# Loading the old state of an mLSTM layer in whole-sequence pieces, one step ahead of its products

## The chip, the core and the metric

The kernel runs on one core of a Trainium2 chip. The metric is the device time of one execution in microseconds (us), the median of a few runs. The engines named below are TensorE (PE, with its weight loads PEld), VectorE (DVE), ScalarE (ACT), GpSimd (POOL) and SyncE (SP), whose queue issues most of the loads from memory.

## What is computed

The reference is one inference step of a two-layer trunk, for a prompt of 512 tokens and 8 sample sequences of 4 tokens (544 columns together): a half-step feed-forward block, a mixer, another half-step block, per layer. The mixer of the first layer is an mLSTM with 4 heads of width 512; that of the second is a chunked gating MLP. What the change touches is one term of the mLSTM, for the 8 sample sequences, which carry an old state C0 of 512x512 per sequence and head:

```python
def _mlstm_chunk(C0, n0, m0, q, k, v, ig, lf):
    ...
    num = (jnp.einsum('bhts,bshe->bthe', sc, v)
           + jnp.einsum('bthd,bhde->bthe', q, C0) * w_inter.transpose(0, 2, 1)[..., None])
    ...
    h = num / den
```

The einsum of q and C0 is what the text calls q C0. For each of 4 heads and 8 sequences it reads 1 MB of state, 32 MB in all.

## The kernel before

Each layer's activations lie as 8 tiles of 128 channels by 544 columns. A large product is made as three products of rounded parts: each weight tile of 128x1024 is loaded into a buffer `raw` (512 KB), split by ACT into a high part `whi` (L274) and by DVE into a low part `wlo` (L275), and then used by 48 products of `mm3` (L260). There are two buffers each of `whi` and `wlo`, and six of `raw` (`RAW = 6`). A `raw` buffer comes free when the split of its tile is done.

The mLSTM has a first phase (`phase_a`) and a second (`phase_b`). The first has 16 steps, one for each tile of the up-projection: step i loads and multiplies the i-th tile of `in_ml_up`, runs the convolution and the small projections of the tile before (`post`), and then pops two jobs from the list `self.units`. The sixteen gate tiles (`z_tile`, the second half of `in_ml_up`, here z0 to z15) follow: z0 at the end of the first phase, the rest as steps `z1` of the second, in an order that is written out by hand. Its beginning, for the first head, is

```python
B_FIRST = ("u2 z1 z1 z1 z1 g1 u1 u2 u1 u1 z1 z1 z1 s1 u2 u1 u1 z1 z1 u2 u2 z1 z1 z1 a3 u1 s1 u1 u2 q0 z1 s1 q1 "
```

where `u1` pops one job of `self.units`, `u2` two, `z1` makes a gate tile, `g1` turns the gate rows into columns (`columns`, L1051 to L1064), `s1` makes a step of the sample part and `q0` one of the prompt part.

`self.units` holds the q C0 work, 19 jobs for each head (`sample_units`, L1137): a `begin` that loads the head's q and lays it out in `qpad` as 4 x 8 tiles of 128x32 columns, two empty jobs, and 16 units. A unit takes one sequence b and half of the state's row tiles: it loads two row tiles of 128x512 (512 KB) into a buffer of the same six as the weights (`c0`, L1152; the trace calls it `c`) and makes two fp32 products (L1157), each with 32 columns of output on a column group of its own (`tile_position=(0, 32 * dt)`). They add up in one PSUM tile over the eight sequences. The last unit of a head also copies the PSUM tile out.

Outside the feed-forward blocks the order of instructions on an engine isn't the order of the program word for word: when the program is built, an instruction whose inputs would not be there yet lets ready ones of its engine go ahead, and a buffer is given to the first in the program that waits for it. Each product of L1157 shows as two records in the trace, since fp32 runs in two passes.

Of the kernel before, what the change touches and what calls it, by code (L numbers as in the profile page):

```python
# [10 lines left out]
F32 = mybir.dt.float32  # L11
# [7 lines left out]
P = 128  # L19
# [11 lines left out]
RAW = 6  # L31
# [148 lines left out]
class Trunk:  # L180
# [956 lines left out]
    def sample_units(self, h):  # L1137

        nc, a = self.nc, self.a
        s = {}  # L1140

        def begin():
            qk = self.mc.tile([P, 4, NS], F32, tag="qu", name="qu", bufs=1)
            nc.sync.dma_start(out=qk, in_=self.aux_d[h][:, :, :NS])
            for e in range(4):
                q = self.qpad[:, e].rearrange("p b t -> p (b t)")
                dg = bass.AP(q.tensor, q.offset, [list(q.ap[0]), [NS + 4, 8], [1, 4]])
                nc.gpsimd.tensor_copy(out=dg, in_=qk[:, e, :].rearrange("p (b t) -> p b t", t=4))
            s["qc"] = self.st()

        def unit(b, d2):
            c0 = self.wp.tile([P, 1024], F32, tag="raw", name="c0", bufs=RAW).rearrange("p (d e) -> p d e", d=2)  # L1152
            dsl = slice(2 * d2 * P, (2 * d2 + 2) * P)
            nc.sync.dma_start(out=c0, in_=a["sC"][b, h, dsl].rearrange("(d p) e -> p d e", p=P))
            for dd in range(2):
                dt = 2 * d2 + dd
                nc.tensor.matmul(out=s["qc"][32 * dt:32 * dt + 32, :], lhsT=self.qpad[:, dt, b, :], rhs=c0[:, dd, :],  # L1157
                                 start=b == 0, stop=b == 7, tile_position=(0, 32 * dt))

        def end():  # L1160
            t = self.com.tile([P, NT], F32, tag="sq", name="qct", bufs=2)[:, :512]
            nc.scalar.activation(out=t, in_=s["qc"], func=AF.Copy)
            nc.scalar.dma_start(out=self.qc_d[h], in_=t)

        jobs = [begin] + 2 * [lambda: None] + [lambda b=b, d2=d2: unit(b, d2) for b in range(8) for d2 in range(2)]

        def last(w=jobs[-1]):
            w()
            end()
        return jobs[:-1] + [last]  # L1170
# [458 lines left out]
```

## Time and profile before

| | us |
|---|---|
| median of 3 runs | 2242.74 |
| lowest run | 2239.98 |
| the profiled execution | 2241.03 |
| its span, first to last instruction | 2239.3 |
| PE busy in the span | 2196.3 |

What lies outside the span is 1.7 us. The highest of the three runs is 7586.79 us, an outlier. Busy times are unions over an engine's instructions; a matmul's end is modelled, so that neighbours overlap a little. In a timeline a row is a stretch of like instructions: start, length, engine, line, shape and how many of them.

### The profile page before, as it was taken

To read this page: it belongs to the slowest core of one execution; us is meant where nothing else is said; L and a number is where in the kernel's file an instruction comes from. 1 tells how busy PE (TensorE), PEld (TensorE's weight loads), DVE (VectorE), ACT (ScalarE), POOL (GpSimd) and SP (SyncE) were. 2 spreads that over 40 slices of the span, in tenths; PEclk is the share of its full clock that TensorE was granted. 3 is DMA by queue.
4 is the path that set the end of the run, shared out by engine and by line. 5 is a ranking of instruction groups with operands and counts; after the bars stand their busy time and mean duration, and the time that the engine had idled before them with its cause. 6 is when DMAs were issued, how large, how long until landed. Compare 5 with 4: busy or idle time off the path is not lost.

```text
span 2239.3 us, 42182 instructions
## 1 busy us (share of the span) xinstructions
PE 2196.3 (98%) x17056; PEld 2096.5 (94%) x17056; DVE 1601.2 (72%) x2271; ACT 1094.1 (49%) x1646; POOL 357.9 (16%) x499
## 2 busy tenths in 40 slices
PE   7999999999999999999999999999999999999997
PEld 7999999888987789899999999999999999999997
DVE  7989887544356676898998756555565567988885
ACT  6655655444455453665655542132224445665654
POOL 0111111332111100011111011121112100111110
PEclk9999999999999999999999999999999999999999
DMA  5677774576767653367777557876874224676772
GB/s 168 158 196 166 174 180 127 177 231 216 260 225 258 222 183 111 83 155 188 167 186 178 149 194 247 291 255 213 294 233 160 79 75 100 159 196 165 177 177 64
DMA packets 176603, 405.17 MB, mean 181 GB/s; under 512 B 18224, under 2 KB 47232, under 8 KB 176408
## 3 DMA queue, kind: packets, MB, share of 16 engines
q1 hardware_dynamic: 119296, 299.10, 41.6%
q0 software_dynamic: 36560, 79.12, 17.4%
q10 hardware_dynamic: 20552, 24.26, 3.0%
q8 instruction: 134, 2.20, 0.4%
q14 instruction: 61, 0.50, 0.1%
HBM read 342.60 MB, written 59.81 MB: 180 GB/s over the span
## 4 chain that ended last, share of the span: by engine, by line
PE 91%; DVE 4%; ACT 2%; DMA 2%; issue 1%; POOL 0%; SPq 0%; POOLq 0%; ACTq 0%; DVEq 0%
PE set L157 44%; PE mm L260 34%; PE mm L1364 2%; PE s L1157 2%; PE s L1327 1%; PE s L1291 1%; PE s L929 1%; PE mm L739 1%; PE s L260 1%; PE s L1550 1%; DMA xs<-xsd 1%; PE s L1478 0%; PE s L1274 0%; DMA vd<-vt 0%; DVE xt L157 0%
## 5 line engine op out<-in xcount | busy, mean ns | idle before, releaser
L274 ACT ACTIVATE whi<-raw 128x1024 fp32r<-128x1024 f32 (+2 forms) x148 | 151.5, 1024 | 468.0 <-PE mm L260 353.9
L260 PE MATMUL mm<-xgh,whi 128*128 128x272 f32 x1616 | 339.7, 291 | 1.0 <-DVE xm L249 1.0
L260 PE MATMUL mm<-xgl,whi 128*128 128x272 f32 x1616 | 335.8, 289 | 1.0 <-DVE xgl L157 0.9
L260 PE MATMUL mm<-xgh,wlo 128*128 128x272 f32 x1616 | 334.4, 288 | 1.3 <-DVE wlo L275 1.3
L157 PE MATMUL set<-xsh,whi 128*128 128x272 f32 x1056 | 305.4, 289 | 12.9 <-ACT whi L157 9.5
L157 PE MATMUL set<-xsl,whi 128*128 128x272 f32 x1056 | 304.4, 288 | 0.9 <-DVE xsl L157 0.9
L157 PE MATMUL set<-xsh,wlo 128*128 128x272 f32 x1056 | 304.2, 288 | 0.8 <-DVE wlo L157 0.8
L157 DVE TENSOR_TENSOR wlo<-raw,whi 128x1024 fp32r<-128x1024 f32 (+2 forms) x205 | 226.8, 1106 | 80.3 <-ACT whi L157 80.2
L260 PEld LDWEIGHTS mm<-xgh,whi 128*128 128x128 f32 x1616 | 254.0, 188 | 19.9 <-issue 15.5
L260 PEld LDWEIGHTS mm<-xgl,whi 128*128 128x128 f32 x1616 | 253.6, 188 | 1.9 <-DVE xgl L157 1.9
L260 PEld LDWEIGHTS mm<-xgh,wlo 128*128 128x128 f32 x1616 | 252.8, 188 | 2.1 <-DVE wlo L275 1.6
L157 ACT ACTIVATE whi<-raw 128x1024 fp32r<-128x1024 f32 (+2 forms) x205 | 197.9, 965 | 81.0 <-PE set L157 68.4
L157 ACT ACTIVATE set<-set 128x272 f32<-128x272 f32 x285 | 108.8, 382 | 239.6 <-PE set L157 235.5
L157 PEld LDWEIGHTS set<-xsh,whi 128*128 128x128 f32 x1056 | 199.0, 188 | 14.0 <-ACT whi L157 9.5
L275 DVE TENSOR_TENSOR wlo<-raw,whi 128x1024 fp32r<-128x1024 f32 (+2 forms) x148 | 176.4, 1192 | 42.5 <-ACT whi L274 39.1
L157 PEld LDWEIGHTS set<-xsh,wlo 128*128 128x128 f32 x1056 | 199.4, 189 | 1.4 <-DVE wlo L157 1.4
L157 PEld LDWEIGHTS set<-xsl,whi 128*128 128x128 f32 x1056 | 199.4, 189 | 1.1 <-DVE xsl L157 1.1
L157 PE MATMUL set<-xsh,whc 128*128 128x272 f32 x584 | 169.8, 291 | 1.6 <-ACT whc L157 1.6
L157 PE MATMUL set<-xsh,wlc 128*128 128x272 f32 x584 | 169.3, 290 | 0.7 <-DVE wlc L157 0.7
L157 PE MATMUL set<-xsl,whc 128*128 128x272 f32 x584 | 169.7, 291 | 0.0
L157 PE MATMUL set<-hl,whi 128*128 128x272 f32 x496 | 143.7, 290 | 0.0
L157 PE MATMUL set<-hh,wlo 128*128 128x272 f32 x496 | 142.9, 288 | 0.0
(387 smaller groups left out, 5363.9 us busy)
## 6 DMA issues: line engine op xcount, KB each, us to landing
raw<-in_ffn_gate SPq DMA_DIRECT2D x88, 512.0 KB
raw<-in_ffn_up SPq DMA_DIRECT2D x88, 512.0 KB
c<-in_sC SPq DMA_DIRECT2D x64, 512.0 KB
c<-in_sC SPq DMA_DIRECT2D x32, 1024.0 KB
out_Cs<-c POOLq DMA_DIRECT2D x32, 1024.0 KB, 6.8
raw<-in_ffn_down SPq DMA_DIRECT2D x80, 384.0 KB
raw<-in_ml_up SPq DMA_DIRECT2D x32, 512.0 KB
raw<-in_ffn_up POOLq DMA_DIRECT2D x60, 256.0 KB, 5.9
```

The costliest lines, as they stand in the source:

```text
L157: r = f(*args, **kw)
L260: nc.tensor.matmul(out=ps[h], lhsT=w[:, wsl], rhs=x[:, h * HN:(h + 1) * HN], start=k == 0 and q == 0, stop=k == n - 1 and q == 2)
L274: nc.scalar.activation(out=hi, in_=src, func=AF.Copy)
L275: nc.vector.tensor_tensor(out=lo, in0=src, in1=hi.bitcast(F32), op=ALU.subtract)
L739: nc.tensor.matmul(out=ps[:, pi, :HN], lhsT=w[:, w0:w0 + P], rhs=h[pi], start=z == 0, stop=z == 6 * nj - 1)
L929: nc.tensor.matmul(out=ps[:, tt * P:(tt + 1) * P], lhsT=t[:, tt * P:(tt + 1) * P], rhs=wd[w], start=True, stop=True)
L1157: nc.tensor.matmul(out=s["qc"][32 * dt:32 * dt + 32, :], lhsT=self.qpad[:, dt, b, :], rhs=c0[:, dd, :], start=b == 0, stop=b == 7, tile_po ...
L1291: nc.tensor.matmul(out=ps[:, :n], lhsT=kk[:, i * P:(i + 1) * P], rhs=qq[:, i * P:NP], start=z == 0, stop=z == 11)
L1327: nc.tensor.matmul(out=ps, lhsT=s_[:, c], rhs=v_[:, i], start=i == 0 and q == 0, stop=i == T and q == 2)
L1364: nc.tensor.matmul(out=ps, lhsT=kk[:, tt], rhs=vv[:, tt], start=tt == 0 and q == 0, stop=tt == 3 and q == 2)
L1550: nc.tensor.matmul(out=ps[r], lhsT=s["ks"][v][rows, dsl], rhs=s["vs"][rows], start=True, stop=True, tile_position=(32 * r, 0))
```

## The change

The 16 units of a head become 8 pairs of jobs, `load` and `unit`, one pair for each sequence. `load` takes two of the six buffers and loads all four row tiles into them; `unit`, the next job in the list, makes the four products, one after the other, on the four column groups. A head still has 19 jobs, so the places in the hand-written order stay; as two jobs are popped in each step of the first phase, a load there stands one step before its unit.

```diff
-        def unit(b, d2):
-            c0 = self.wp.tile([P, 1024], F32, tag="raw", name="c0", bufs=RAW).rearrange("p (d e) -> p d e", d=2)
-            dsl = slice(2 * d2 * P, (2 * d2 + 2) * P)
-            nc.sync.dma_start(out=c0, in_=a["sC"][b, h, dsl].rearrange("(d p) e -> p d e", p=P))
-            for dd in range(2):
-                dt = 2 * d2 + dd
-                nc.tensor.matmul(out=s["qc"][32 * dt:32 * dt + 32, :], lhsT=self.qpad[:, dt, b, :], rhs=c0[:, dd, :],
+        def load(b):
+            s["c0"] = []
+            for d2 in range(2):
+                c0 = self.wp.tile([P, 1024], F32, tag="raw", name="c0", bufs=RAW).rearrange("p (d e) -> p d e", d=2)
+                dsl = slice(2 * d2 * P, (2 * d2 + 2) * P)
+                nc.sync.dma_start(out=c0, in_=a["sC"][b, h, dsl].rearrange("(d p) e -> p d e", p=P))
+                s["c0"] += [c0[:, 0, :], c0[:, 1, :]]
+
+        def unit(b):
+
+            for dt, c0 in enumerate(s["c0"]):
+                nc.tensor.matmul(out=s["qc"][32 * dt:32 * dt + 32, :], lhsT=self.qpad[:, dt, b, :], rhs=c0,
                                  start=b == 0, stop=b == 7, tile_position=(0, 32 * dt))
...
-        jobs = [begin] + 2 * [lambda: None] + [lambda b=b, d2=d2: unit(b, d2) for b in range(8) for d2 in range(2)]
+        jobs = [begin] + 2 * [lambda: None] + [lambda f=f, b=b: f(b) for b in range(8) for f in (load, unit)]
```

## Rows read from the trace of the kernel before

**Rows 1.** The page's busy times of PE and PEld over the span, the slices of PE and of the granted clock, and the two heads of the chain that ended last, by engine and by line.

```profile
PE 2196.3 (98%) x17056; PEld 2096.5 (94%) x17056; DVE 1601.2 (72%) x2271; ACT 1094.1 (49%) x1646; POOL 357.9 (16%) x499
...
PEclk9999999999999999999999999999999999999999
...
PE 91%; DVE 4%; ACT 2%; DMA 2%; issue 1%; POOL 0%; SPq 0%; POOLq 0%; ACTq 0%; DVEq 0%
```

**Rows 2.** Busy time of each engine in two stretches that hold all of the q C0 products, first of all instructions, then of line 1157 alone. Columns: length, then busy us and instructions of each engine, granted clock, share of the DMA engines, GB/s.

```profile
425.00:560.00 135.00, 134.49 (x1119) 112.75 (x1119) 62.25 (x113) 58.81 (x82) 41.21 (x103) 1.00 0.69 221
560.00:800.00 240.00, 237.14 (x1653) 195.54 (x1653) 134.03 (x277) 115.05 (x198) 31.53 (x62) 0.99 0.70 235
...
425.00:560.00 135.00, 13.85 (x80) 2.36 (x80) 1.00 0.69 221
560.00:800.00 240.00, 27.88 (x176) 5.46 (x176) 0.99 0.70 235
sum 375.00, PE 41.73 PEld 7.82; mean PE 20.86 PEld 3.91
```

**Rows 3.** Whom PE waited for from 425 to 800 us: us in total, times, longest.

```profile
PE s L1327 <- ACT hn L1330: 2.1, 1, 2.1
PE mm L1364 <- ACT cst L1367: 0.7, 1, 0.7
PE s L1157 <- POOL qpad L1148: 0.5, 1, 0.5
```

**Rows 4.** PE's timeline at six places: stretches of q C0 records (line 1157) of different length, for three of them with what follows.

```profile
687.69 1.04 PE L1157 MATMUL s<-c,qpad 128*32 128x512 f32 x2
...
513.89 1.05 PE L1157 MATMUL s<-c,qpad 128*32 128x512 f32 x4
...
441.46 1.06 PE L1157 MATMUL s<-c,qpad 128*32 128x512 f32 x8
442.46 0.52 PE L260 MATMUL mm<-xgh,whi 128*128 128x272 f32 x2
...
451.24 1.06 PE L1157 MATMUL s<-c,qpad 128*32 128x512 f32 x8
452.23 0.52 PE L260 MATMUL mm<-xgh,whi 128*128 128x272 f32 x2
...
461.69 1.04 PE L1157 MATMUL s<-c,qpad 128*32 128x512 f32 x6
462.66 0.44 PE L949 MATMUL s<-con,qkvs 128*128 128x128 f32 x2
463.03 1.04 PE L1157 MATMUL s<-c,qpad 128*32 128x512 f32 x2
464.01 0.52 PE L260 MATMUL mm<-xgh,whi 128*128 128x272 f32 x2
...
741.42 1.92 PE L1157 MATMUL s<-c,qpad 128*32 128x512 f32 x16
```

**Rows 5.** One step of the first phase: SP's issues of weight tiles and state pieces, and the split of the weight tile that was issued at 442.58 us (ACT for the high part, DVE for the low one). What PE does at 452.23 and 464.01 stands in the group above.

```profile
441.12 0.37 SPq L1154 DMA_DIRECT2D c<-in_sC  x1
442.58 0.34 SPq L212 DMA_DIRECT2D raw<-in_ml_up  x1
443.01 8.24 SPq L1154 DMA_DIRECT2D c<-in_sC  x2
452.33 0.34 SPq L212 DMA_DIRECT2D raw<-in_ml_up  x1
...
448.54 1.06 ACT L274 ACTIVATE whi<-raw 128x1024 fp32r<-128x1024 f32 x1 [4.23 <-PE mm L260]
...
449.63 1.23 DVE L275 TENSOR_TENSOR wlo<-raw,whi 128x1024 fp32r<-128x1024 f32 x1
```

**Rows 6.** The place in the second phase around `g1`: SP's issues, the two splits by ACT and by DVE, and PE from the last gate-row transposes to the next gate tile.

```profile
543.26 14.00 SPq L1154 DMA_DIRECT2D c<-in_sC  x4
562.77 0.34 SPq L212 DMA_DIRECT2D raw<-in_ml_up  x1
...
569.83 0.33 SPq L212 DMA_DIRECT2D raw<-in_ml_up  x1
...
567.48 1.06 ACT L274 ACTIVATE whi<-raw 128x1024 fp32r<-128x1024 f32 x1 [0.46 <-ACT sz L1113]
...
561.54 1.20 DVE L275 TENSOR_TENSOR wlo<-raw,whi 128x1024 fp32r<-128x1024 f32 x1
...
568.58 1.23 DVE L275 TENSOR_TENSOR wlo<-raw,whi 128x1024 fp32r<-128x1024 f32 x1 [2.26 <-ACT whi L274]
...
571.36 0.38 PE L1059 MATMUL s<-con,r_rep 4*128 4x4 f32 x4
571.67 2.77 PE L1157 MATMUL s<-c,qpad 128*32 128x512 f32 x20
574.37 0.52 PE L260 MATMUL mm<-xgh,whi 128*128 128x272 f32 x2
```

**Rows 7.** Whom SP's queue waited for, in the whole span: its state pieces (L1154) and its weight tiles (L212), us in total, times, longest.

```profile
SPq L1154 <- DVE wlo L275: 62.8, 19, 9.9
...
SPq L1154 <- PE s L1157: 19.7, 9, 4.2
...
SPq L212 <- PE s L1157: 10.8, 9, 3.1
```

## The prediction

> **What bounds the kernel now.** I read the page's busy times first: PE works 2196.3 of 2239.3 us, at full clock, and holds 91% of the chain that ended last [rows 1]. Then the two stretches with the q C0 products: from 425 to 560 us PE is busy 134.49 of 135 us, from 560 to 800 us 237.14 of 240 [rows 2]. Its only waits there are 2.1, 0.7 and 0.5 us [rows 3]. So in these 375 us PE is the bound but for 3.3 us, and a change can gain only what it takes off PE's own list. What it can lose is a new wait of PE, and SP's queue shows where that could come from: state pieces wait for the split of a weight tile, and weight tiles wait for q C0 products [rows 7]. They share six buffers.
>
> **What the change takes off PE.** All q C0 records keep PE busy 41.73 us, 13.85 in the first phase and 27.88 in the second [rows 2]. How long a stretch lasts hardly depends on how many column groups are at work: one product (x2) takes 1.04 us, two (x4) 1.05, four (x8) 1.06, and eight (x16) 1.92, or 0.96 for each four [rows 4]. So a stretch costs about 1 us for each four products on different groups, and the same for one or two. The change makes every four products of a sequence stand together: 4 heads x 8 sequences = 32 quartets. If each stands alone that is 32 x 1.06 = 33.9 us; if they stand in pairs as in the x16 row, 32 x 0.96 = 30.7. The gain is 41.73 - 33.9 = 7.8 us, at most 11.0. I take 7.8, because in the first phase, where the order is regular, one quartet stands at the end of each step, as the x8 rows do.
>
> Most quartets are there already. In the first phase two units were popped in a step, the second half of one sequence and the first half of the next, and they are on four different groups: x8 in 1.06 us [rows 4]. 64 units each alone would be 64 x 1.05 = 67 us and not 41.73. What is lost now is in the odd stretches: the single half units at either end of a head, the x6 and x2 around a transpose, the lone x2 and x4 of the second phase. By phase: ten units lie in the first, 13.85 - 10 x 1.06 = 3.3 us; 22 in the second, 27.88 - 22 x 1.06 = 4.6.
>
> The Trainium skill, TensorEngine Tiling, Theoretical Speedup, gives up to 4x for outputs of at most 32 columns. Read as two groups before and four after, that would halve the whole 41.73 us (the last rival); the trace disagrees, since it shows four groups at work already.
>
> PE's number of products, weight loads and bytes stays: 64 loads of 512 KB, one PSUM tile per head. SP issues the same 64. Those edits cost nothing by themselves.
>
> **What the change moves: the buffers.** I count the six `raw` buffers through the trace in program order (weight tile, piece, piece). It explains when SP issues: the pieces and weight tiles at 442.58 and 443.01 leave after the products at 441.46, that at 452.33 after those at 451.24 [rows 4, 5]; the tile at 562.77 leaves when the split that began at 561.54 ends, 1.20 us later [rows 6]. So a load waits for the release of a buffer and all later ones queue behind it on SP.
>
> First phase. Now a piece is released in the step of its load. After the change the two buffers of a sequence are held from one step's end to the next step's end, so the release that lets a weight tile go comes one step later. A step is 452.23 - 442.46 = 9.8 us. Now the tile issued at 442.58 is split from 448.54 to 450.86 and used at 464.01: it is ready 13.2 us early [rows 4, 5]. Issued one step later, right after the quartet at a step's end, it has 5.96 us to the split as here, and 2.32 for the split: ready 8.3 us after the issue, which comes 0.1 us into a step, and needed at the next one's start, 9.7 after. 1.4 us of cover is left, so I cost it at nothing. ACT's split keeps its place inside the step. If the tile lands 2 us later, the cover is gone (the slower rival).
>
> Second phase, at `g1`. Now five pieces wait in buffers while z1 to z4 run, and the sixth buffer takes the tile of z5, at 562.77 [rows 6]; PE goes through the five units (x20, 2.77 us) and finds z5 ready at 574.37. After the change, the jobs `u1 u2 u1 u1` at this place are load, unit and load, unit, load (24 jobs are popped in the first phase and two by the first `u2`, which leaves a load in front). The three loads are six pieces: they take all six buffers, and z5's tile must wait for the first quartet after `g1`. Call its start T. Its buffers come free at T + 1.1. From issue to the end of the split the same tile now takes 568.58 + 1.23 - 562.77 = 7.0 us [rows 6]: z5 is ready at T + 8.1. Until then PE has the two quartets of this place and, as its pieces are there, the third, 3 x 0.96 = 2.9 us. PE can begin on the high part 1.2 us before the low one is done, but only its first products (some 0.5 us) need no low part. The new wait is 8.1 - 2.9 - 0.5 = 4.7 us, and I take 5. Bounds: 0, if ready work of the sample part fills it (or the order built leaves a buffer for z5); 7, if the third quartet doesn't go ahead (1 us) and the tiles of z6 and z7, issued with it, share the transfer (1 us). What is queued behind z5's tile on SP are the next tiles and small loads of the sample and prompt parts, none of which PE touches within the next 9 us now, so they cost nothing more. After that the buffers turn over as before.
>
> Elsewhere in the second phase loads and units stand close, and SP runs ahead as buffers allow. No wait of PE in this stretch is for a weight tile or a piece now [rows 3], so other ready work covers late loads there. I put it at 0, between a gain of 3 (the quartets go in pairs) and a loss of 5 (one more such wait).
>
> **Sum.** 2241.03 (the profiled execution) - 7.8 + 5 = 2238.2 us. The median of the runs before is 1.7 above that execution; I put the median after at 2239.
>
> **The rivals.**
> *The whole gain.* The wait at `g1` is filled or doesn't arise: -7.8 to -11.0, 2230 to 2233. For it: PE's only waits now are short, the order is built to fill holes. Against: six pieces are six buffers.
> *Weight tiles late in the first phase (slower).* Place: each step from the ninth to the sixteenth, PE before its first product of L260. Price: the cover is 1.4 us; one more piece in front of a tile is 512 KB at the stretch's 221 GB/s [rows 2], 2.4 us; 1.0 us lost in each of eight steps is 8, and 2 us each is 16. With the 5 at `g1`: -7.8 + 5 + 8 to 16 = +5 to +13, 2246 to 2254. It decides from an issue-to-split time of 7.4 us, against 5.96 now. For it: one release now lets two or three loads go at once. Against: in the rows a tile is already issued within 1.5 us of two pieces, and still is split after 5.96 us.
>
> The Trainium skill, DMA: Bandwidth & Descriptors, Queues, rings and completion order, says that descriptors are consumed in ring order on each engine; by that a tile pays for every piece in front of it in SP's queue, which speaks for this rival. No row here separates a tile alone from one behind two pieces.
>
> *It doesn't do what it says.* Transposes or other ready products go between a quartet's products, as the x6 and x2 show now [rows 4], and stretches of fewer than four products stay: gain 3 or less, and the wait at `g1` comes: 2243 to 2246.
> *Half of all q C0 time.* If each product now ran beside one other and then beside three, 41.73 / 2 = 20.9 us would go, 2220. Against: the x8 rows, which run four at once now [rows 4].
>
> **Chances and range.** Forecast (2234 to 2242) 0.45, the whole gain 0.2, late weight tiles 0.23, not what it says 0.1, half of the q C0 time 0.01, several waits like that at `g1` 0.01. For 8 in 10 that is 2229 to 2253: from the lower end of the whole gain, up into the late weight tiles, whose upper end and the last two cases are left out. Two per cent is 44.9 us, about what a measurement of this kernel can tell from no change. Faster by that would need more than the 41.73 us of all q C0 products; slower needs nine waits like that at `g1`. So 0.01 faster, 0.97 the same, 0.02 slower.
>
> **What would show it.** PE busy at the line of the products near 34 us (31 to 34), nearly all stretches x8 or multiples; ten of them up to z1. A wait of PE of some 5 us before z5, for DVE's low part or ACT's high part, and SP's z5 issue just behind the first quartet after `g1`. Weight tiles split one step later, with no wait of PE before them. Wrong would make it: waits of PE for `whi` in every step; no wait at `g1`; a q C0 time still near 40 us.

## The result and the profile after

The changed kernel takes 2256.34 us (median of 4 runs, 2254.68 to 2259.64) against 2241.69 for the kernel before: a ratio of 1.007, with a 95% interval from 1.005 to 1.009. It is slower by 14.7 us or 0.7%. The profiled execution took 2255.45 us, 14.4 more than that of before. Of the 2% classes that is no change, as forecast; the forecast time, 2239, and its upper end, 2253, were both too low. In the lines of the changed kernel the products are L1162 and the loads of the pieces L1156; what stood behind the units has moved by five lines.

The page first: busy times of PE and PEld over a span of 2253.7 us, and the chain that ended last by engine.

```profile
PE 2199.6 (98%) x17056; PEld 2101.4 (93%) x17056; DVE 1602.6 (71%) x2271; ACT 1093.0 (48%) x1646; POOL 347.9 (15%) x499
...
PE 86%; DMA 4%; DVE 4%; ACT 3%; issue 2%; POOL 0%; SPq 0%; POOLq 0%; ACTq 0%; DVEq 0%
```

PE has 91 - 86 = 5% less of the chain than before; DMA has 2% more, ACT and issue 1% each [rows 1]. PE stands idle for 2253.7 - 2199.6 = 54.1 us, where it stood 43.0 before: 11.1 of the 14.4 us. The other 3.3 are more busy time, though PE has as many instructions as before.

The same two stretches as in [rows 2], the second one made 30 us longer since all is later now; first all instructions, then the q C0 products alone (columns as there).

```profile
425.00:560.00 135.00, 134.61 (x1131) 113.86 (x1130) 64.49 (x115) 60.40 (x84) 33.24 (x104) 1.00 0.69 221
560.00:830.00 270.00, 253.53 (x1760) 211.39 (x1759) 147.19 (x304) 119.28 (x209) 32.44 (x63) 0.97 0.66 222
...
425.00:560.00 135.00, 12.66 (x80) 2.08 (x80) 1.00 0.69 221
560.00:830.00 270.00, 25.52 (x176) 4.40 (x176) 0.97 0.66 222
sum 405.00, PE 38.19 PEld 6.48; mean PE 19.09 PEld 3.24
```

The q C0 products are busy for 38.19 us, 3.5 less than before; I had forecast 33.9. The first stretch is as full as it was. PE's new idle time lies in the second: it is idle there for 270 - 253.53 = 16.5 us. Its waits say for what (from 425 to 830 us; us in total, times, longest):

```profile
PE mm L260 <- ACT whi L274: 9.4, 1, 9.4
PE s L1197 <- DVE hl L275: 2.2, 1, 2.2
```

With seven smaller ones (1.8 us and less) they come to 16.9 us, against 3.3 before [rows 3]. One is the forecast wait before z5, at 9.4 us where I had put 5. The others, some 4 us more than before, I had put at nothing.

The place around `g1`, engine by engine: SP's issues, with the last two of the four `xs` loads once more by themselves, PE from the first quartet behind `g1` to z5, and ACT up to the split of z5 (start, length, engine, line, how many; in brackets the idle time before and what ended it).

```profile
540.71 19.87 SPq L1156 DMA_DIRECT2D c<-in_sC  x5
...
562.22 9.94 SPq L1377 DMA_DIRECT2D xs<-xsd  x4
...
571.21 0.95 SPq L1377 DMA_DIRECT2D xs<-xsd  x2
...
572.25 2.53 SPq L212 DMA_DIRECT2D raw<-in_ml_up  x3
...
569.12 1.92 PE L1162 MATMUL s<-c,qpad 128*32 128x512 f32 x16
...
571.06 0.63 PE L1162 MATMUL s<-c,qpad 128*32 128x512 f32 x3
...
571.12 1.02 PE L1162 MATMUL s<-c,qpad 128*32 128x512 f32 x5
581.52 0.82 PE L260 MATMUL mm<-xgh,whi 128*128 128x272 f32 x2 [9.38 <-ACT whi L274]
...
576.96 0.75 ACT L1378 ACTIVATE xs<-xs,cols 128x544 f32<-128x544 f32 x1 [5.36 <-DMA xs<-xsd]
...
578.27 1.28 ACT L1200 ACT_TABLE_LOAD   x1
...
579.79 0.73 ACT L1378 ACTIVATE xs<-xs,cols 128x544 f32<-128x544 f32 x1
580.43 1.99 ACT L274 ACTIVATE whi<-raw 128x1024 fp32r<-128x1024 f32 x2
```

The quartets begin at T = 569.12. PE does all three at once (x16, x3 and x5 are 24 records, or 12 products), as forecast, and is through them at 571.12 + 1.02 = 572.14. z5's weight tile leaves SP only at 572.25, 3.1 us after T and not 1.1: four loads of head 0's gated output (`xs`, L1377) stand before it on the queue, and the last two don't leave until 571.2 us; SP's queue waits up to 8.1 us there for the store of what they read. Then ACT doesn't take the split up when the tile is there. It works in the order in which it was built; it waits for the third of those loads until 576.96, scales it (L1378), does a gate and a table load, scales the fourth, and splits z5 at 580.43. That is 8.2 us from issue to split, where it was 4.7 [rows 6].

The wait has a second price. Around it, all engines (columns as in [rows 2]):

```profile
560.00:569.00 9.00, 9.00 (x81) 8.85 (x79) 3.76 (x10) 3.16 (x6) 3.21 (x5) 1.00 0.76 234
573.00:581.50 8.50, 0.00 (x0) 0.00 (x0) 0.19 (x2) 4.51 (x7) 0.38 (x1) 0.69 0.91 346
581.50:584.00 2.50, 2.48 (x9) 2.17 (x10) 2.36 (x2) 0.92 (x1) 0.00 (x0) 0.50 1.05 403
584.00:586.00 2.00, 2.00 (x11) 2.00 (x10) 0.00 (x0) 0.00 (x0) 0.00 (x0) 0.50 1.06 394
586.00:588.00 2.00, 2.00 (x16) 2.00 (x15) 0.00 (x0) 0.00 (x0) 0.00 (x0) 0.89 1.04 394
```

PE was busy at a granted clock of 1.00 (2.4 GHz), then idle, and z5's products begin at 0.50 (1.2 GHz). In 4.5 us at 0.50 and 2 us at 0.89 they lose 4.5 x 0.50 + 2 x 0.11 = 2.5 us, which the page counts as busy. The Trainium skill, TensorE: Matmul & The Clock Gate, What's actually happening, says that the array is throttled unless its own activity releases it; the trace agrees, at 0.50 after the idle stretch.

### The profile page after: what moved, and what is told of

Read it like the earlier page. It is cut to its first block, busy times and chain, and to the rows that moved or that the text cites. A ratio compares the mean times of both kernels' runs of the same rounds, so it can differ in the third digit from the quotient of the medians.

```text
span 2253.7 us, 42180 instructions
## 1 busy us (share of the span) xinstructions
PE 2199.6 (98%) x17056; PEld 2101.4 (93%) x17056; DVE 1602.6 (71%) x2271; ACT 1093.0 (48%) x1646; POOL 347.9 (15%) x499
## 4 chain that ended last, share of the span: by engine, by line
PE 86%; DMA 4%; DVE 4%; ACT 3%; issue 2%; POOL 0%; SPq 0%; POOLq 0%; ACTq 0%; DVEq 0%
PE set L157 45%; PE mm L260 31%; DMA xs<-xsd 2%; PE mm L1369 1%; PE s L1332 1%; PE s L929 1%; PE s L1162 1%; DMA kv<-kvsd 1%; PE s L1296 1%; PE mm L739 1%; PE s L1555 1%; PE s L260 1%; PE s L1483 0%; PE s L910 0%; DMA out_Cs<-c 0%
## 5 line engine op out<-in xcount | busy, mean ns | idle before, releaser
L260 PE MATMUL mm<-xgh,whi 128*128 128x272 f32 x1616 | 340.5, 292 | 11.1 <-ACT whi L274 10.1
L260 PE MATMUL mm<-xgl,whi 128*128 128x272 f32 x1616 | 336.5, 289 | 1.5 <-DVE xgl L157 1.4
L260 PE MATMUL mm<-xgh,wlo 128*128 128x272 f32 x1616 | 335.0, 289 | 1.3 <-DVE wlo L275 1.3
L260 PEld LDWEIGHTS mm<-xgh,whi 128*128 128x128 f32 x1616 | 254.7, 189 | 29.1 <-ACT whi L274 13.3
L260 PEld LDWEIGHTS mm<-xgh,wlo 128*128 128x128 f32 x1616 | 253.4, 188 | 3.3 <-DVE wlo L275 1.9
L260 PEld LDWEIGHTS mm<-xgl,whi 128*128 128x128 f32 x1616 | 254.3, 189 | 2.4 <-DVE xgl L157 2.4
```

The source lines that it names most:

```text
L260: nc.tensor.matmul(out=ps[h], lhsT=w[:, wsl], rhs=x[:, h * HN:(h + 1) * HN], start=k == 0 and q == 0, stop=k == n - 1 and q == 2)
```

## Experiments

Every ratio is to the kernel before on the same chip, with its 95% interval; the median of before lay between 2238.0 and 2240.7 us there.

**The order of the jobs (e1_order).** The job that makes the third load stands behind the gate tiles:

```diff
-... g1 u1 u2 u1 u1 z1 z1 z1 s1 u2 u1 u1 z1 z1 u2 u2 ...
+... g1 u1 u2 u1 z1 z1 z1 s1 u1 u2 u1 u1 z1 z1 u2 u2 ...
```

> Edit: in the hand-written order of the first head the last load of the g1 group (the fifth sequence's two pieces) goes behind z5, z6, z7 and the sample step. All else is the changed kernel. Theory G (all six buffers are held by pieces when z5's weight tile is wanted): only four pieces stand before z5's tile, it is loaded while z4 runs, PE's 9.4 us wait before z5 and the slow clock after it (z5 takes 8.5 us instead of 6.2) are gone: 2256.3 - 9.4 - 2.3 = 2244 to 2246 us. Rival L (the loss is spread over the second phase, from releases that come late everywhere; the g1 wait only collects it): the wait moves to a later gate tile, 2252 or more. Rival H (the q C0 products as such cost more in the second phase): within 3 us of 2256.

Measured: 1.0061 (1.0047 to 1.0075). There is no wait before z5. Instead six pieces now stand before z8, three gate tiles later. SP's and PE's timeline there, and PE's first wait in the list:

```profile
578.93 9.45 SPq L1156 DMA_DIRECT2D c<-in_sC  x6
...
595.11 0.81 SPq L212 DMA_DIRECT2D raw<-in_ml_up  x2
...
594.04 2.74 PE L1162 MATMUL s<-c,qpad 128*32 128x512 f32 x21
...
PE mm L260 <- ACT whi L274: 4.2, 1, 4.2
```

Six loads leave, then no weight tile until the quartet at 594.04 has let two buffers go; the tile leaves 1.07 us after that quartet's start. The wait moved with the sixth piece. By its number this run is what the text calls rival L (2252 or more), and not the 2244 to 2246 of theory G; e5 below tells the two apart, since no wait comes back there.

**A seventh buffer (e2_seven, e3_before_seven).** `RAW = 7`, in the changed kernel and in the kernel before.

> Edit: seven raw buffers instead of six in the changed kernel. Theory G: z5's weight tile has the seventh, its wait is gone, as in the kernel with the moved load: 2244 to 2246 us, less what seven buffers give the kernel before too. Rival L: the wait gets shorter by part, 2250. Rival H: no change, 2256.

> Edit: seven raw buffers instead of six in the kernel before, as the control of the other run with seven. Theory G: PE has no wait for a weight tile in the second phase of the kernel before, so a seventh buffer gives nothing: 2241 to 2243 us. Rival L: buffers are short in general and the seventh gives some us here too, 2236 or less.

Measured: 1.0026 (1.0015 to 1.0037) with the change, 1.0005 (0.9996 to 1.0014) without. The wait before z5 is gone, and so is most of the loss. The buffer itself is worth nothing to the kernel before. But the change is not below 1 either: in the first phase PE now waits at L942 for ACT's `vt`, 4.1 us in two waits.

**Load and products in one job (e4_one_job).** The quartets stay, but nothing is held from one job to the next:

```diff
-jobs = ... [lambda f=f, b=b: f(b) for b in range(8) for f in (load, unit)]
+jobs = ... [lambda f=f, b=b: f(b) for b in range(8) for f in (both, none)]
```

> Edit: load and products of a sequence stand in one job, the second job of the pair is empty; nothing is loaded one step ahead, the quartets stay. Theory G: the three sequences of the g1 group still stand before z5 in the program, so their six pieces still take all six buffers and the wait stays: 2254 to 2258 us. Rival A (holding pieces from one job to the next is the cause): the wait goes, 2246 or less. In the first phase weight tiles go back to being split a step earlier, which was covered either way.

Measured: 1.0048 (1.0036 to 1.0061). (Here and in e6 the lines behind the jobs stand seven further on.) The wait before z5 stays, at 10.2 us, since the job in front of the gate tiles still loads six pieces. The later waits nearly go: 1.9 and 1.4 us are the only others. The time lies between what the two theories gave. So the wait at `g1` comes from six pieces in six buffers, not from loading one job ahead; that seems to have a price of its own (1.0048 against 1.007), which e5 to e7 look at.

**No more than four pieces ahead (e5_four_ahead, e6_four_one_job).** The order is rewritten so that never more than four pieces stand before a run of gate tiles, with the change as it is (e5) and with the single job of e4 (e6):

```diff
-... g1 u1 u2 u1 u1 z1 z1 z1 s1 u2 u1 u1 z1 z1 u2 u2 ...
+... g1 u1 u2 u1 z1 z1 z1 s1 u1 u2 u1 z1 z1 u1 u2 u2 ...
```

> Edit: the changed kernel with the first head's order rewritten so that no more than two sequences (four pieces) stand between one run of gate tiles and the next: before z5, before z8 and before z10. Theory G (a weight tile waits where six pieces stand before it): no wait of PE at z5 or z8, no slow clock, 2256.3 less 9.4 and 2.4: 2243 to 2246 us. Rival L (buffers are short all along, each repair moves the wait on): another wait of 4 us or more at z10 or later, 2250 or more.

> Edit: the same rewritten order, with load and products in one job and the second job empty. Theory G: the kernel with one job had the wait at z5 (10.2 us, and the slow clock) and nothing else against it; without it 2249.3 - 12: 2236 to 2239 us, below the kernel before. If holding pieces costs nothing by itself, it is as fast as the run with loads one step ahead, 2243 to 2246.

Measured: e5 1.0029 (1.0017 to 1.0041), e6 1.0011 (0.9998 to 1.0023). In neither does PE wait for a weight tile. PE's longest waits from 425 to 830 us, of e5:

```profile
PE s L1197 <- DVE hl L275: 2.6, 1, 2.6
PE s L942 <- ACT vt L932: 2.2, 2, 1.5
```

and of e6, with its q C0 time in the stretches of [rows 2]:

```profile
PE s L1339 <- ACT hn L1342: 3.8, 1, 3.8
...
sum 405.00, PE 36.17 PEld 6.87; mean PE 18.09 PEld 3.43
```

e6 is the change without the wait and without the holding: its q C0 products take 5.6 us less of PE than before, and it was expected to be faster for that (2236 to 2239 us). It is not, at 1.0011 of the kernel before. Part of it is seen: the end of the last head waits 3.8 us for ACT's `hn`, where it waited 2.1 before [rows 3].

**The order alone (e12_before_order).** The kernel before with the order of e5 and e6.

> Edit: the kernel before, half units and all, in the rewritten order of the first head. It is the control of the two runs with that order. If the order is neutral by itself, 2238 to 2243 us, ratio 0.999 to 1.001, and the 3 to 5 us that those runs differ by are the loads held one step ahead. If the order gains or costs by itself, the ratio shows how much of theirs is the order's.

Measured: 0.9991 (0.9981 to 1.0000). The rewritten order costs nothing, so what e5 loses it doesn't lose to that. It is also the nearer control of e6, which has the same order and stands 1.0011 - 0.9991 = 0.0020, or 4.5 us, above it, with intervals that just overlap. The wait for `hn` at the end of the last head is 1.0 us here and 3.8 in e6.

**The change in heads 0 and 1 only (e7_heads01).** Heads 2 and 3 keep the old half units.

> Edit: the change for the first two heads alone; the other two keep the half units of the kernel before. Theory G with a second part (holding pieces one job ahead costs some 4 us in the second phase's later heads, from 660 us on): the wait at z5 stays and the later part is gone: 2250 to 2253 us. If all of the loss is at z5, within 2 us of 2256.

Measured: 1.0052 (1.0040 to 1.0064). The wait before z5 stays at 10.0 us, and beside it PE waits for 1.5, 0.9 and 0.2 us only.

**What held z5's split (e8_out_load_pool, e9_two_out_loads).** In e8 GpSimd issues the third and fourth `xs` load of head 0 in SP's place. In e9 `xs` has two buffers and not four, so that these two loads come later in the order of SP and of ACT.

> Edit: the third and fourth output load of the first head (L1377, in front of z5's tile on SP's queue) are issued by GpSimd. Nothing else is reordered. If the extra 2 us between the release of the buffers and the issue of z5's tile are SP's queue, the tile leaves at the release, 2 us earlier, and PE's wait before z5 falls from 9.4 to about 7: 2253 to 2254 us. If ScalarE's order holds the split (it scales those two tiles before it splits z5's), the tile lands earlier but the wait stays within 1 us of 9.4 or grows: 2255 to 2258.

> Edit: the changed kernel with two buffers instead of four for the output loads (tile xs), so that the first head's third and fourth load and their scaling on ScalarE no longer stand before z5's split. What the prediction costed (tile issued at the release, 1.1 us after the first quartet's start, and 7.0 us from issue to the end of the split) should then be seen: PE waits 4.5 to 6 us before z5 instead of 9.4, and the total is 2250 to 2253 us if later output loads lose nothing by the two buffers. If the wait stays near 9 us, the transfer itself is slow here, with three weight tiles and three pieces in flight.

Measured: e8 1.0091 (1.0077 to 1.0106), e9 1.0124 (1.0103 to 1.0145). e8 around `g1` (first quartet, tile, ACT, z5):

```profile
570.25 1.92 PE L1162 MATMUL s<-c,qpad 128*32 128x512 f32 x16
...
571.34 1.30 SPq L212 DMA_DIRECT2D raw<-in_ml_up  x3
...
582.19 0.75 ACT L1378 ACTIVATE xs<-xs,cols 128x544 f32<-128x544 f32 x1 [9.76 <-DMA xs<-xsd]
585.66 1.99 ACT L274 ACTIVATE whi<-raw 128x1024 fp32r<-128x1024 f32 x2
...
586.75 0.82 PE L260 MATMUL mm<-xgh,whi 128*128 128x272 f32 x2 [13.49 <-ACT whi L274]
```

With SP's queue clear the tile leaves 1.09 us after T, as the prediction has it; but ACT stands 9.76 us before the scaling of an `xs` load that comes later still, and the tile's split behind it. So ACT's order alone is enough to hold the split. In e9, where that scaling is out of the way too, with the clock of z5's first products:

```profile
569.34 1.92 PE L1162 MATMUL s<-c,qpad 128*32 128x512 f32 x16
...
570.43 1.28 SPq L212 DMA_DIRECT2D raw<-in_ml_up  x3
...
575.26 1.98 ACT L274 ACTIVATE whi<-raw 128x1024 fp32r<-128x1024 f32 x2
...
576.35 0.82 PE L260 MATMUL mm<-xgh,whi 128*128 128x272 f32 x2 [3.99 <-ACT whi L274]
...
576.30:579.50 3.20, 3.15 (x12) 2.85 (x13) 2.36 (x2) 0.94 (x1) 0.00 (x0) 0.50 0.78 204
```

Issue at T + 1.09, split 4.8 us later, a wait of 4.0 us: close to the working of the prediction (4.7). The kernel as a whole is slower all the same. Up to 830 us PE's waits come to 11.4 us, less than the changed kernel's 16.9, though two of them, 2.3 and 1.9 us for DVE's `hns`, are new. What it loses, it loses behind 830 us; the longest of PE's waits there up to 1350 us:

```profile
PE mm L1369 <- ACT cst L1372: 4.7, 1, 4.7
```

The changed kernel waits 0.5 us at that line there. PE's granted clock is lower too, 0.97 from 870 to 1000 us and 0.89 from 1300 to 1345, against 0.99 and 1.00. That the two buffers are the cause is likely, as nothing else was changed, but the chain from them to these waits was not followed.

**What PE's time is worth (e10_half_products).** The kernel before without the q C0 products of the odd sequences; the loads stay.

```diff
-            for dd in range(2):
+            for dd in range(0 if b % 2 else 2):
...
-                                 start=b == 0, stop=b == 7, tile_position=(0, 32 * dt))
+                                 start=b == 0, stop=b == 6, tile_position=(0, 32 * dt))
```

> Edit: the kernel before without the q C0 products of the odd sequences (their loads stay); the sample's outputs miss these terms. It measures what time taken off PE is worth. If PE bounds these 375 us all the way, the total falls by what the products' busy time falls (about half of 41.7 us: 2220 to 2225 us). If ends of chains absorb part of it, as a wait before the last head's L1327 does, the fall is smaller than the busy time taken away, by several us.

Measured: 0.9988 (0.9973 to 1.0003), 2234.81 us against 2238.42. The products' busy time in the stretches of [rows 2], and PE's first waits there:

```profile
sum 405.00, PE 23.30 PEld 3.81; mean PE 11.65 PEld 1.90
...
PE s L1291 <- ACT hs L1219: 4.4, 1, 4.4
PE s L1274 <- DVE hns L1230: 2.3, 1, 2.3
```

18.4 us less work on PE, and the median is 3.6 us lower; the interval goes from 6 us faster to 1 us slower, so that even 3.6 is not clear of the noise, but 18.4 is ruled out. The waits from 425 to 830 us grow from 3.3 [rows 3] to 11.7 us, for steps of the sample part on ACT and DVE that stand close behind PE. That leaves 10 of the 18.4 us. The profiled execution was in fact 8.1 us below that median of before, but its twelve runs spread from 2228.56 to 2242.26, nine of them above the profiled one by 2 us or more; where the rest goes in those these rows don't show.

**The change again (e11_after_again),** on the chip of e9 and e10.

> The changed kernel itself, beside the others on one chip. Both theories: 14 to 16 us over the kernel before, ratio 1.006 to 1.007.

Measured: 1.0083 (1.0064 to 1.0102). The wait before z5 is 8.8 us in this execution, that at L1197 3.3.

## Why the prediction was wrong, step by step

**The buffers at `g1`: the wait came as described, its price was too small.** Six pieces take all six buffers, z5's tile leaves behind the first quartet, the third quartet goes ahead, and PE then waits: all as the prediction says. e1, e2 and e5 show that it is the count of pieces, since the wait moves with the sixth piece and goes with a seventh buffer or with four pieces. The term was 5 us and is 9.4 of waiting plus 2.5 of slow clock, 11.9. z5 was to start at T + 7.6 and started at T + 12.4. The step that failed is "none of which PE touches within the next 9 us now, so they cost nothing more": I looked at what is queued behind the tile, and not at what stands before it, 2.0 us on SP (T + 3.1 for T + 1.1) and 3.5 us on ACT (8.2 us to the split for 4.7). A step that goes ahead of the tile when the tile is late is not seen in a trace where the tile is early. Even the bound of 7 us fell, as it held only PE's and the transfer's share, and the slow clock behind the wait was in no term at all. e8 and e9 show what ACT's share does: it grows when the loads before the tile come later, and with them out of the way the wait is 4.0 us, near the 4.7 of the working. In time, e5 against the changed kernel and its second run gives 1.007 - 1.0029 to 1.0083 - 1.0029, or 9 to 12 us, for this place.

**The quartets: 7.8 us forecast, 3.5 measured off PE, and no gain that the time shows.** Two steps failed. That every quartet stands unbroken did not hold everywhere. In the first phase two of the ten still come as x2 and x6 around a transpose, at 458.7 and 500.2 us, which is 2 us of the 12.66. Near the end of the mLSTM, from PE's timeline:

```profile
778.94 1.04 PE L1162 MATMUL s<-c,qpad 128*32 128x512 f32 x2
782.17 0.34 PE L1197 MATMUL s<-qks 128*32 128x32 f32 x5 [2.19 <-DVE hl L275]
782.33 0.63 PE L1162 MATMUL s<-c,qpad 128*32 128x512 f32 x3
782.78 0.60 PE L1162 MATMUL s<-c,qpad 128*32 128x512 f32 x3
784.76 1.05 PE L1162 MATMUL s<-c,qpad 128*32 128x512 f32 x2
...
790.97 1.06 PE L1162 MATMUL s<-c,qpad 128*32 128x512 f32 x6
```

Two quartets, 16 records, come out as x2, x3, x3, x2 and x6, with products of the sample part between them (PE even waits 2.2 us for one of these inside the first), and take about 4.2 us of PE where two unbroken ones take 2 x 1.06 = 2.1. That was the rival that it doesn't do what it says, which I gave 0.1. It holds for 4.3 of the 7.8 us: 1.2 was gained in the first phase of 3.3, and 2.4 of 4.6 in the second. And "a change can gain only what it takes off PE's own list" names a bound, but I took it as the price. e10 takes 18.4 us off and gains 3.6 in the median; e6 takes 5.6 off and gains none. PE at 98% with waits of 3.3 us told that PE is bound now; it didn't tell how far behind the next chain is. e10's waits put ACT's and DVE's ends of the sample part close behind; that is seen for 8.4 of its 18.4 us, and argued for the rest.

**Elsewhere in the second phase: 0 forecast, about 4 us measured.** That is within its bounds (-3 to +5), but at the end of them. Three pairs point the same way: e5 against e6 (1.0029 and 1.0011, 4 us), the changed kernel against e4 (1.007 and 1.0048, 5 us), and against e7 (1.007 and 1.0052, 4 us). With the change's second run (1.0083) the last two are 8 and 7 us, beyond the bounds. In each pair the intervals overlap, and the last two also compare different chips, each by its ratio to before, so each alone is weak. What they share is that pieces are held one job ahead in the later heads; and e5 and the changed kernel both have a wait at L1197 for DVE's `hl` (2.6 and 2.2 us) that e4, e6 and e7 don't have. But e2 and e9 hold pieces too and have no such wait, so holding alone doesn't make it. Just before `hl`, in the changed kernel:

```profile
780.16 0.75 ACT L1378 ACTIVATE xs<-xs,cols 128x544 f32<-128x544 f32 x1 [1.38 <-DMA xs<-xsd]
780.82 1.06 ACT L274 ACTIVATE hh<-s 128x512 fp32r<-128x512 f32 x2
```

`hh` is what DVE needs for `hl`, and ACT splits it off only after it has waited for an `xs` load, as at `g1`; it waits 1.52 us there in e5 and 2.51 in e11. No run moved this load alone, so that it is the cause is not shown, and what held the load up stays open.

**The first phase: right, though its working was not.** No wait of PE before L260 there, which refutes the rival of late weight tiles. SP, ACT, DVE and PE of one step:

```profile
439.60 0.34 SPq L212 DMA_DIRECT2D raw<-in_ml_up  x1
...
444.15 1.06 ACT L274 ACTIVATE whi<-raw 128x1024 fp32r<-128x1024 f32 x1 [3.17 <-DMA raw<-in_ml_up]
...
445.24 1.22 DVE L275 TENSOR_TENSOR wlo<-raw,whi 128x1024 fp32r<-128x1024 f32 x1 [5.02 <-ACT whi L274]
...
449.25 0.52 PE L260 MATMUL mm<-xgh,whi 128*128 128x272 f32 x2
```

The tile leaves just behind the quartet that begins at 438.48, as forecast, and its split begins 4.6 us later, not 5.96. It is ready at 445.24 + 1.22 = 446.46 and used at 449.25: 2.8 us of cover, where I had 1.4. The row in front of me said why: the split in [rows 5] was released by PE, which gave `whi` back, so that 5.96 us was no landing time. Here ACT waits for the DMA itself.

**The sum.** Forecast -7.8 + 5 + 0 = -2.8 us. (From the profiled execution's 2238.2 the 1.7 us to the median would have given 2239.9; 2239 was put down.) Measured, by the pairs: no gain for the quartets; with the first run 9 for the place at `g1` and 4 to 5 elsewhere, 13 to 14 for a loss of 14.7 (1.007); with the second 12 and 7 to 8, 19 to 20 for a loss of 18.6 (1.0083). By the profiled executions: PE idle +11.1; PE busy +3.3, which is -3.5 from the quartets, +2.5 from the clock behind z5, and 4.3 that is not placed. In e11, the same kernel, PE is busy for 2196.8 us, 2.8 less, so most of these 4.3 is what two executions can differ by. No version tried is shown to be faster than the kernel before; the lowest with the change and all its work is e6, whose interval holds 1.

## What to carry to other kernels

Before tiles are held longer in a shared ring, count its buffers through the program up to each place where another user of the ring follows, and find the place where they are all taken; the job order that was safe with five pieces here was not with six. For the tile that comes late there, list what stands in front of its load on the queue and in front of its first use on each engine that works in order, not only what stands behind. And price microseconds taken off a busy engine by leaving work out in one run, before counting them as gained.

## What the hardware showed that I had not expected

A wait of PE costs more than its length: behind 9.4, 4.2 (e1, granted 0.60 and 0.54 in the first 4 us) and 4.0 us of waiting, the next products began at the lower clock, 2.5 us more in the first case. The kernel before has this too, behind the 2.1 us of [rows 3]: 0.53 from 795.6 to 799.2 us. And 18.4 us of fp32 products could be left out of an engine that is 98% busy for a gain of 3.6 us in 2238, at most 6 by the interval.
